# Hybrid mLSTM and neighbourhood-attention block on one core: low parts by accumulating DMAs and no elementwise work on POOL, from w_b to the feed forward

## The chip, the cores and the metric

The kernel runs on one core of one Trainium2 chip. The metric is device time in microseconds for one execution of the whole program, as the median of the executions shown. A core has TensorE (PE; its weight loads are listed as PEld), VectorE (DVE), ScalarE (ACT), GpSimd (POOL) and SyncE (SP), and DMA queues that SP and POOL issue to. All of them run on their own and wait for each other through semaphores.

## The reference, cut to what matters

One encoder layer on 1024 tokens of width 1024 and 16 meta tokens ahead of them. The projection `u = rms_norm(h) @ w_in` feeds two mixers, a bidirectional mLSTM (result y_a, 1024 wide) and a neighbourhood attention (result y_b, 512 wide), and the gates g_a and g_b. The change touches what comes after:

```python
mix = g_a * (y_a @ w_branch_a) + g_b * (y_b @ w_branch_b)
h = h + mix @ w_out
z = rms_norm(h, norm2_g) @ w_ff1            # 1024 -> 4096
h = h + jnp.square(jax.nn.relu(z)) @ w_ff2  # 4096 -> 1024
```

Everything is float32.

## The kernel before

**Three products for one.** Each operand of a matmul is kept as a high part, a copy rounded to the format of the fast matmul, and a low part, the operand less its high part. `mm3` multiplies high by high, high by low and low by high into one PSUM bank. The helper `hilo` makes both parts: ACT copies the high part, and `rest` subtracts it from the source on VectorE or POOL, whichever a running account of both (`either`, with the weight `share_gp`) calls free sooner. `gp_helps` allows POOL in this choice; it is false until the mixers are done and true from there on. In the mixers and in `Weights`, for w_in and w_b, low parts are made otherwise: ACT copies the high part with its sign turned, and a DMA issued by POOL adds the source to it in place.

**Stages.** They run in this order: w_b (eight column blocks `w_b[j]`, 24 matmuls each, by `gemm_in`, with the evacuation `ev_b` on VectorE, which multiplies by the gate tile gbq); w_a (four objects `Cols`, `cols_a`); w_out (one object `Rows`, `out_p`); w_ff1 (sixteen `Cols`, `cols_1`); w_ff2 (four `Rows`, `rows_2`). `Cols` and `Rows` form each product of 2 by 2 blocks with seven block products in place of eight, so sums and differences of blocks are made first. The blocks of the activations are A11, A12, A22 and the sums S1 to S4 (`s_parts`); for w_a they are the y operands, 14 pairs of high and low tiles of 128 x 1024. `ASIDE` says which one belongs to which of the seven products. A `Cols` step is 12 matmuls with 512 columns, a `Rows` step 24. A column of `Cols` reads its weights into two raw tiles (r0, r1), for w_a from a pool of three buffers ("wr"), and makes seven parts c1 to c7 of them, each 512 columns high and 512 low.

**Order.** The list `seq` holds all steps. For each step `ensure` first prepares operands up to `ah` steps ahead (`AH1` is 5, in w_out `AH2` is 2), and hooks in `before` issue loads. In the first ten steps of w_ff1 (the products 1 and 2 of five columns, `NE2`), which use the first half of the activations only, the look-ahead shrinks to the last of these steps. The second half, h21 and h22, passes norm2, the transposes `zt` and `s_parts` in that time. The tile framework schedules the instructions of each engine with a timeline of its own, so an instruction may stand earlier than its place in the program. Nearly all tiles are slots of one pool of 44 (`NSLOT`).

**Around the change.** `load_gb` reads the gate tiles gbq back from DRAM for w_b; ev_b's result goes to DRAM (gbd) and is read again as gba for w_a's evacuation `out_a`. The evacuation of w_ff1, `out_1`, adds two results and then takes max(z, 0) * z in one VectorE instruction. The weights of w_out are the tiles wo; their parts are called pow01 to pow17, those of the mix poz01 to poz17 (quarter, then product). Parts of w_a are wa0c to wa3c, of w_ff1 w10c to w115c. Most instructions are issued by the wrapper in line 137 and so carry this line.

Of the kernel before, what the change touches and what calls it, by code (L numbers as in the profile page):

```python
# [17 lines left out]
S = 1024  # L18
# [164 lines left out]
def build(tc, A, taps=None):  # L183
# [49 lines left out]
    def rest(out, src, part, bulk=1.0):  # L233
        either(free(out), bulk).tensor_sub(out, src, part.bitcast(F32))
# [879 lines left out]

    W.split_to(([*w_ga.values()] + w_b)[GS])
    nsp.close()
    gp_helps[0] = True
    LP = ctx.enter_context(tc.tile_pool(name="late", bufs=1))

    def late(name, dt=F32):  # L1120
# [13 lines left out]
    def add(out, a, b):  # L1134
        either(free(out), share_gp[0]).tensor_add(out, a, b)

    def hilo(src, name):
        h_, l_ = slot(name + "h", F32R), slot(name + "l", F32R)
        SC.copy(h_[:, 0:S], src[:, 0:S])
        rest(l_[:, 0:S], src[:, 0:S], h_[:, 0:S], share_gp[0])  # L1140
        return h_, l_


    gbd = dp.tile([4, 2, 128, 1024], F32, name="gbd")
    ybs = []
    for j in range(8):
        if f"ga{j}" not in F.done:
            F.add(f"ga{j}", job_ga(j), GE)
    for u in range(4):
        F.fill(12)  # L1150
        ybs.append(hilo(yb[u], f"yb{u}"))
    while F.jobs:
        F.fill(12)

    gb = {}

    def load_gb(p):
        for h_ in range(2):
            gb[p, h_] = slot(f"gbq{p}{h_}")
            dma(gb[p, h_][:, 0:1024].rearrange("p (e t) -> p e t", e=2),  # L1160
                gated[2 * p:2 * p + 2, :, h_ * 512:h_ * 512 + 512].rearrange("e p t -> p e t"))

    def ev_b(j):
        def ev(b, n0, n, ps):
# [10 lines left out]

    ASIDE = {1: "A11", 2: "A12", 3: "S4", 4: "A22", 5: "S1", 6: "S2", 7: "S3"}

    def s_parts(q, z, name):

        s1 = [slot(f"{name}s1{i}") for i in range(2)]  # L1180
        for i in range(2):
            add(s1[i][:, 0:S], q[1, i][:, 0:S], q[1, 2 + i][:, 0:S])
            z["S1", i] = hilo(s1[i], f"{name}s1{i}")
        yield
        for i in range(2):
            a11, a21 = q[0, i], q[1, i]
            sub(a21[:, 0:S], a11[:, 0:S], a21[:, 0:S])
            sub(a11[:, 0:S], s1[i][:, 0:S], a11[:, 0:S])
            z["S2", i] = hilo(a11, f"{name}s2{i}")
        yield  # L1190
        for i in range(2):
            z["S3", i] = hilo(q[1, i], f"{name}s3{i}")
        yield
        for i in range(2):
            z["A22", i] = hilo(q[1, 2 + i], f"{name}a22{i}")
        yield
        for i in range(2):
            sub(q[0, 2 + i][:, 0:S], q[0, 2 + i][:, 0:S], q[0, i][:, 0:S])
            z["S4", i] = hilo(q[0, 2 + i], f"{name}s4{i}")
        yield  # L1200

    LATE_C = (("w10", 1), ("w10", 2), ("w11", 1))
# [1 line left out]
    class Cols:  # L1204


        def __init__(self, name, src, z, out, raw_slot):
            self.name, self.src, self.z, self.out, self.raw_slot = name, src, z, out, raw_slot
            self.r, self.c, self.t = {}, {}, {}
            self.gen = self.parts()  # L1210

# [5 lines left out]
                self.r[e] = t  # L1217
            return self.r[e]

        def part(self, i, src):  # L1220
            c = late("c", F32R) if (self.name, i) in LATE_C else slot(f"{self.name}c{i}", F32R)
            SC.copy(c[:, 0:512], src)
            rest(c[:, 512:1024], src, c[:, 0:512], share_gp[0])
            self.c[i] = c

        def parts(self):
            e = self.raw(0)
            b11, b21 = e[:, 0:512], e[:, 512:1024]
            self.part(1, b11)
            yield  # L1230
            self.part(2, b21)
            yield
            o = self.raw(1)
            b12, b22 = o[:, 0:512], o[:, 512:1024]
            tt = late("tt")
            t1, t2 = tt[:, 0:512], tt[:, 512:1024]
            sub(t1, b12, b11)
            sub(t2, b22, t1)
            self.part(6, t2)
            yield  # L1240
# [49 lines left out]
    class Rows:  # L1290


        def __init__(self, name, quarters, out, tmp):
            self.name, self.quarters, self.out, self.tmp = name, quarters, out, tmp
            self.q, self.z, self.w = {}, {}, {}
            self.gen = {}

# [3 lines left out]

        def part(self, q, i, a, b, da=None, db=None):
            self.z[q, i] = self.split(a, da, f"{self.name}z{q}{i}")
            self.w[q, i] = self.split(b, db, f"{self.name}w{q}{i}")

        def split(self, t, src, name):
            if src is None:
# [8 lines left out]
        def parts(self, q):  # L1316
            self.load(q)
            c = slice(0, 1024)
            (a11, a12, a21, a22), (b11, b12, b21, b22) = [[t[:, c] for t, _ in x] for x in self.q[q]]
            (_, _, _, d22), (_, _, e21, e22) = [[src for _, src in x] for x in self.q[q]]  # L1320
            self.q[q] = None
            self.part(q, 1, a11, b11)
            yield
            self.part(q, 2, a12, b21, None, e21)
            yield
            s1, t1 = self.tmp("s1")[:, c], self.tmp("t1")[:, c]
            add(s1, a21, a22)
# [52 lines left out]
    def out_a(p):  # L1380
        def out(h_, e, ps, addend):
            g, b = ga[p, h_][:, lo(e)], gb[p, h_][:, lo(e)]
            c = cols_a[p].spare()[:, 512:1024]
            V.tensor_add(c, ps, addend)
            V.scalar_tensor_tensor(g, g, 1.0, c, OP.add, OP.mult)
            V.scalar_tensor_tensor(g, b, 2.0, g, OP.mult, OP.add)
        return out

    cols_a = [Cols(f"wa{p}", A["w_a"][2 * p:2 * p + 2], za, out_a(p), False) for p in range(4)]
    sy = s_parts(yq, za, "y")  # L1390
    NBS = ((0, 512), (512, 512))
    load_gb(0)
    for j in range(8):
        if j == 7:
            cols_a[0].prep(2, 0)
        if j % 2 == 0 and j < 6:
            load_gb(j // 2 + 1)
        run(gemm_in(w_b[j], NBS, ev_b(j), 4, ([t[0] for t in ybs], [t[1] for t in ybs])))
        if j in (1, 2):
            load_ya(j - 1)  # L1400
        if j in (3, 4):
            for i in (0, 1):
                za["A11" if j == 3 else "A12", i] = hilo(yq[0, 2 * (j - 3) + i], f"ya{j}{i}")
        if j >= 5:
            next(sy)
    ybs = None
# [31 lines left out]
    def out_quarters(q):  # L1438
        a = [(ga[p, h_], None) for p, h_ in ((q, 0), (2 + q, 0), (q, 1), (2 + q, 1))]
        b = []  # L1440
        for kh in range(2):
            for ch in range(2):
                t = slot(f"wo{q}{kh}{ch}")
                dma(t[:, 0:1024], A["w_out"][kh * 2 + q, ch])
                b.append((t, None))
        return a, b

    def load_x2(t):
# [38 lines left out]
        dma(h2d[t * 128:(t + 1) * 128, :], hx[t][:, 0:D])  # L1487
        norm2(t)

    out_p = Rows("po", out_quarters, out_o, late)  # L1490


    z2d = dp.tile([16, 2, 128, 1024], F32, name="z2d")
# [1 line left out]
    def out_1(p):  # L1495
        zq, cnt = {}, [0, 0]

        def out(h_, e, ps, addend):
            if h_ not in zq:
                zq[h_] = slot(f"zq{p}{h_}")  # L1500
            o = zq[h_][:, lo(e)]
            V.tensor_add(o, ps, addend)
            V.scalar_tensor_tensor(o, o, 0.0, o, OP.max, OP.mult)
            cnt[h_] += 1
            if cnt[h_] == 2:
                dma(z2d[p, h_], zq.pop(h_)[:, 0:1024])
        return out
# [77 lines left out]
    def hook(d, n, fn):  # L1585
        d.setdefault(n, []).append(fn)
# [41 lines left out]
        hook(before, n_1 + 2 * k + 3, lambda: next(sz))  # L1628
    for p in range(16):
        n = next(k for k, x in enumerate(seq) if x[0] is cols_1[p] and x[1] == (6 if p < NE2 else 1))  # L1630
        hook(before, n - 7 if p >= NE2 else max(n - 5, n_1 + 2 * NE2), lambda p=p: (cols_1[p].raw(0), cols_1[p].raw(1)))
    for g in range(1, NG):
        for q in range(2):
            hook(before, n_2 + 14 * g - 7 + 3 * q, lambda g=g, q=q: rows_2[g].load(q))
# [3 lines left out]
    for n, (o, i, q) in enumerate(seq):  # L1638
        for fn in before.get(n, ()):
            fn()  # L1640
        share_gp[0] = 1e6 if n >= n_2 - 8 else BULK if n >= n_1 + 2 * NE2 + 14 else 1.5 if n < n_1 else 1.0
        ah = AH3 if n >= n_2 else AH2 if n_o <= n < n_1 - 6 else AH1
        if n_1 <= n < n_1 + 2 * NE2:
            ah = n_1 + 2 * NE2 - 1 - n
        ensure(n + ah, n)
        o.mul(i, q)
    ctx.close()
# [69 lines left out]
```

## Time and profile before

| | us |
|---|---|
| median of 3 runs | 1671.81 (1669.5 to 1674.51) |
| profiled execution, its own time | 1675.85 |
| its span, first to last instruction | 1674.1 |
| TensorE busy | 1607.5 (96%) |
| VectorE busy | 1187.1 (71%) |
| ACT busy | 805.4 (48%) |
| POOL busy | 421.9 (25%) |
| mean granted TensorE clock | 0.984 |

The profile is of one execution. Its times count from the first instruction. Busy shares are means over stages that differ, so a stage is read from a stretch of the span. A matmul's record overlaps the next one's, so a busy TensorE can still lose time to a lower clock; matmuls in a stretch are counted for that.

### The profile page before, as it was taken

What the parts mean: (1) busy time and instruction counts of PE and PEld (TensorE: products, weight loads), DVE (VectorE), ACT (ScalarE), POOL (GpSimd) and SP (SyncE); (2) the same over time, 40 slices, a digit from 0 to 9 for tenths busy, and PEclk for the clock granted to TensorE, in tenths of its full rate; (3) what the DMA queues carried; (4) which work ended last, traced back from release to release, by engine and by line L of the source; (5) the groups of instructions that cost most, each with busy time, mean ns of one, the idle gap of its engine ahead of it and who ended that gap; (6) DMA issues with size and microseconds to landing.
All of it is one profiled execution on the core that took longest, in us unless ns stands there. A gap on an engine that the chain in (4) does not pass through costs nothing.

```text
span 1674.1 us, 22348 instructions
## 1 busy us (share of the span) xinstructions
PE 1607.5 (96%) x8009; PEld 1360.8 (81%) x8009; DVE 1187.1 (71%) x2156; ACT 805.4 (48%) x1418; POOL 421.9 (25%) x480
## 2 busy tenths in 40 slices
PE   6999899999999999999899889799999999999999
PEld 6978789888989989888678668588888887888887
DVE  3537666474757786873588998986667686869597
ACT  5466676576737676753232345322222237353450
POOL 5010212122133313212467565640000000010100
PEclk9999999999999999999999999899999999999999
DMA  6252754636274534446835311033223558281823
GB/s 204 59 133 64 159 135 128 138 87 163 55 188 89 120 69 102 91 105 174 256 106 215 112 70 69 25 137 127 101 101 126 195 170 269 58 264 53 237 77 100
DMA packets 76687, 214.77 MB, mean 128 GB/s; under 512 B 11145, under 2 KB 21769, under 8 KB 76577
## 3 DMA queue, kind: packets, MB, share of 16 engines
q1 hardware_dynamic: 54688, 137.71, 23.6%
q0 software_dynamic: 21888, 75.64, 21.7%
q8 instruction: 63, 1.03, 0.2%
q14 instruction: 48, 0.39, 0.1%
HBM read 166.02 MB, written 38.76 MB: 122 GB/s over the span
## 4 chain that ended last, share of the span: by engine, by line
PE 75%; DVE 9%; DMA 6%; issue 5%; ACT 4%; POOL 1%; SPq 0%; POOLq 0%; DVEq 0%; ACTq 0%
PE pf L137 38%; PE g L137 26%; DMA wl<-w_in 3%; PE po L137 2%; PE pt L137 1%; DVE ga L137 1%; PE pp L137 1%; PE ps L137 1%; PE pu L137 1%; PE pi L137 1%; PE pn L137 1%; DMA gbd<-gbq 1%; DVE zq L137 1%; DVE gt L137 1%; DMA xcl<-xc 1%
## 5 line engine op out<-in xcount | busy, mean ns | idle before, releaser
L137 PE MATMUL g<-xh,wh 128*128 128x512 f32 (+3 forms) x832 | 308.2, 371 | 8.2 <-ACT xm L137 3.0
L137 PE MATMUL g<-xh,wl 128*128 128x512 f32 (+3 forms) x832 | 298.0, 366 | 8.4 <-DMA wl<-w_in 8.4
L137 PE MATMUL g<-xl,wh 128*128 128x512 f32 (+3 forms) x832 | 303.7, 365 | 0.0
L137 PEld LDWEIGHTS g<-xh,wh 128*128 128x128 f32 x832 | 159.5, 192 | 26.7 <-ACT xm L137 3.8
L137 PEld LDWEIGHTS g<-xh,wl 128*128 128x128 f32 x832 | 157.6, 191 | 28.7 <-DMA wl<-w_in 10.3
L137 PEld LDWEIGHTS g<-xl,wh 128*128 128x128 f32 x832 | 159.7, 192 | 16.8
L137 DVE TENSOR_TENSOR acc<-acc,pf 128x512 f32<-128x512 f32 x96 | 64.3, 684 | 39.3 <-PE pf L137 39.2
L174 POOL DMA_DIRECT2D wl<-w_in x44 | 40.5, 920 | 162.4 <-ACT wl L137 71.9
L137 DVE CUSTOM_DVE_ANT_0 P<-ps,bt 128x400 f32<-128x400 f32 x64 | 36.1, 570 | 43.4 <-PE pp L137 20.9
L137 ACT ACTIVATE wl<-wh 128x1024 fp32r<-128x1024 f32 (+1 forms) x52 | 51.4, 989 | 24.7 <-PE g L137 11.6
L137 ACT COPY pu<-pf 128x512 f32<-128x512 f32 x20 | 11.7, 585 | 105.6 <-PE pf L137 105.6
L137 DVE SCALAR_TENSOR_TENSOR C<-C,decb,pu 128x258 f32<-128x258 f32 x52 | 23.7, 479 | 38.0 <-PE pu L137 37.6
L137 DVE SCALAR_TENSOR_TENSOR zq<-zq 128x512 f32<-128x512 f32 x64 | 47.5, 744 | 0.6
L137 ACT ACTIVATE P<-P,mn 128x400 f32<-128x400 f32 x64 | 40.3, 630 | 12.9 <-DVE mn L137 12.4
L137 DVE TENSOR_TENSOR pu<-pf,pu 128x512 f32<-128x512 f32 x40 | 27.3, 684 | 20.6 <-PE pf L137 20.5
L161 POOL DMA_DIRECT2D wh<-w_in x44 | 29.7, 676 | 44.8 <-PE pk L137 16.5
L137 DVE TENSOR_TENSOR zq<-pf,pu 128x512 f32<-128x512 f32 x32 | 22.0, 687 | 25.1 <-PE pf L137 25.1
L137 DVE TENSOR_SCALAR P<-P,sm 128x384 f32<-128x384 f32 (+1 forms) x128 | 38.6, 365 | 0.9
L137 DVE TENSOR_TENSOR zq<-pf,sp 128x512 f32<-128x512 f32 x32 | 22.0, 687 | 22.6 <-PE pf L137 22.4
L137 DVE TENSOR_TENSOR ptl<-pp,pth 128x384 fp32r<-128x384 f32 x64 | 35.5, 555 | 2.6 <-ACT pth L137 1.7
L137 POOL COPY bt<-mbias 128x32 f32<-128x32 f32 x32 | 8.3, 260 | 113.2 <-DVE mn L137 113.1
L137 ACT CAST pth<-pp 128x512 fp32r<-128x512 f32 x60 | 34.0, 581 | 5.4 <-PE pp L137 5.2
(2398 smaller groups left out, 4893.9 us busy)
## 6 DMA issues: line engine op xcount, KB each, us to landing
wh<-w_in POOLq DMA_DIRECT2D x44, 512.0 KB, 5.4
wl<-w_in POOLq DMA_DIRECT2D x44, 512.0 KB, 6.4
z2d<-zq SPq DMA_DIRECT2D x32, 512.0 KB, 3.6
zr<-z2d SPq DMA_DIRECT2D x32, 512.0 KB, 4.5
w2r<-w_ff SPq DMA_DIRECT2D x32, 512.0 KB, 13.2
bt<-rpbd SPq DMA_DIRECT2D x256, 32.0 KB, 2.8
xcl<-xc POOLq DMA_DIRECT2D x8, 520.0 KB, 5.2
ra<-rowd SPq DMA_DIRECT2D x8, 512.0 KB, 4.5
```

The source lines that it names most:

```text
L137: return fn(out, *a, **k)
L161: self.nc.gpsimd.dma_start(h[:, 0:src.shape[-1]], src)
L174: self.nc.gpsimd.dma_start(l[:, 0:w], src, accum_op=OP.add)
```

## The change

From w_b on POOL no longer takes part in additions and subtractions: `gp_helps` stays false, so `either` always answers VectorE. The low parts of the 14 y operands, of all parts of w_a and of all weight parts of w_out are made by ACT (copy of the high part with its sign turned) and an accumulating DMA that POOL issues, from SBUF or, where the tile is changed later, from DRAM. The squares of w_ff1 become two ACT passes. The gate tiles are loaded earlier: the first pair before the last jobs of the mixers, the others one block sooner. The raw tiles of the first two columns of w_ff1 are hooked 6 and 3 steps sooner, and in the early steps of w_ff1 at least two steps are prepared ahead. The low parts of the yb operands, of the mix, of z and of w_ff1 stay subtractions, now on VectorE.

```diff
-    gp_helps[0] = True
...
-    def hilo(src, name):
+    def hilo(src, name, by_dma=False):
         h_, l_ = slot(name + "h", F32R), slot(name + "l", F32R)
         SC.copy(h_[:, 0:S], src[:, 0:S])
-        rest(l_[:, 0:S], src[:, 0:S], h_[:, 0:S], share_gp[0])
+        low(l_[:, 0:S], src[:, 0:S], h_[:, 0:S], by_dma)
         return h_, l_
 
+    def low(l_, src, h_, by_dma):
+        if by_dma:
+
+            SC.activation(l_, h_.bitcast(F32), AF.Copy, scale=-1.0)
+            nc.gpsimd.dma_start(l_, src, accum_op=OP.add)
+        else:
+            rest(l_, src, h_, share_gp[0])
...
+    load_gb(0)
+    while F.jobs:
+        F.fill(12)
...
-        def part(self, i, src):
+        def part(self, i, src, dram=None):
             c = late("c", F32R) if (self.name, i) in LATE_C else slot(f"{self.name}c{i}", F32R)
             SC.copy(c[:, 0:512], src)
-            rest(c[:, 512:1024], src, c[:, 0:512], share_gp[0])
+            low(c[:, 512:1024], src if dram is None else dram, c[:, 0:512], self.by_dma)
...
-            self.w[q, i] = self.split(b, db, f"{self.name}w{q}{i}")
+            self.w[q, i] = self.split(b, b if self.by_dma and db is None else db, f"{self.name}w{q}{i}")
...
-    cols_a = [Cols(f"wa{p}", A["w_a"][2 * p:2 * p + 2], za, out_a(p), False) for p in range(4)]
-    sy = s_parts(yq, za, "y")
+    cols_a = [Cols(f"wa{p}", A["w_a"][2 * p:2 * p + 2], za, out_a(p), False, True) for p in range(4)]
+    sy = s_parts(yq, za, "y", True)
     NBS = ((0, 512), (512, 512))
-    load_gb(0)
+    load_gb(1)
...
-        if j % 2 == 0 and j < 6:
-            load_gb(j // 2 + 1)
+        if j in (1, 3):
+            load_gb(j // 2 + 2)
...
-                za["A11" if j == 3 else "A12", i] = hilo(yq[0, 2 * (j - 3) + i], f"ya{j}{i}")
+                za["A11" if j == 3 else "A12", i] = hilo(yq[0, 2 * (j - 3) + i], f"ya{j}{i}", True)
...
-    out_p = Rows("po", out_quarters, out_o, late)
+    out_p = Rows("po", out_quarters, out_o, late, True)
...
-            V.scalar_tensor_tensor(o, o, 0.0, o, OP.max, OP.mult)
+            SC.activation(o, o, AF.Relu)
+            SC.activation(o, o, AF.Square)
...
-        hook(before, n - 7 if p >= NE2 else max(n - 5, n_1 + 2 * NE2), lambda p=p: (cols_1[p].raw(0), cols_1[p].raw(1)))
+        hook(before, n - 7 if p >= NE2 else max(n - 5, n_1 + 2 * NE2 - (6 if p == 0 else 3 if p == 1 else 0)), lambda p=p: (cols_1[p].raw(0), cols_1[p].raw(1)))
...
-            ah = n_1 + 2 * NE2 - 1 - n
+            ah = max(n_1 + 2 * NE2 - 1 - n, 2)
```

## Rows read from the trace of the kernel before

**Rows 1.** The page: busy time, DMA queues, costliest groups (busy us, mean ns | idle).

```profile
PE 1607.5 (96%) x8009; PEld 1360.8 (81%) x8009; DVE 1187.1 (71%) x2156; ACT 805.4 (48%) x1418; POOL 421.9 (25%) x480
...
q1 hardware_dynamic: 54688, 137.71, 23.6%
q0 software_dynamic: 21888, 75.64, 21.7%
...
L174 POOL DMA_DIRECT2D wl<-w_in x44 | 40.5, 920 | 162.4 <-ACT wl L137 71.9
...
L137 ACT ACTIVATE wl<-wh 128x1024 fp32r<-128x1024 f32 (+1 forms) x52 | 51.4, 989 | 24.7 <-PE g L137 11.6
...
L137 DVE SCALAR_TENSOR_TENSOR zq<-zq 128x512 f32<-128x512 f32 x64 | 47.5, 744 | 0.6
```

**Rows 2.** Busy time by stretch: us, each engine, PEclk, DMA share, GB/s.

```profile
791.84:846.28 54.44, 48.96 (x193) 37.37 (x192) 29.14 (x28) 15.99 (x20) 26.07 (x18) 0.94 0.73 230
846.28:866.83 20.55, 20.25 (x86) 15.40 (x85) 18.97 (x16) 8.69 (x13) 14.18 (x9) 1.00 0.51 176
866.83:925.17 58.34, 58.34 (x253) 47.33 (x252) 51.76 (x55) 15.09 (x25) 40.41 (x23) 1.00 0.51 189
925.17:1026.81 101.64, 90.97 (x373) 70.91 (x372) 94.75 (x83) 44.64 (x59) 63.02 (x36) 0.93 0.20 75
1026.81:1082.32 55.51, 45.60 (x185) 34.64 (x184) 49.95 (x39) 23.16 (x34) 34.16 (x21) 0.88 0.10 38
1082.32:1380.00 297.68, 297.68 (x1288) 241.69 (x1287) 217.60 (x318) 73.61 (x123) 40.08 (x27) 1.00 0.38 135
```

**Rows 3.** The chain that ended last, transposes at the end of w_out (start, us, what).

```profile
1012.30 2.62 PE pt L137 x24
```

**Rows 4.** Waits of TensorE from 791.84 to 1083 (us in total, times, longest).

```profile
PE pf L137 <- DVE zq L137: 5.7, 2, 3.6
...
PE pf L137 <- ACT w10c L137: 2.9, 1, 2.9
```

**Rows 5.** Timeline of POOL and VectorE in w_out (start, us, what).

```profile
938.18 2.42 POOL L137 TENSOR_TENSOR pow12l<-wo,pow12h 128x1024 fp32r<-128x1024 f32 x1 [6.50 <-ACT pow12h L137]
...
936.54 1.22 DVE L137 TENSOR_TENSOR pow11l<-wo,pow11h 128x1024 fp32r<-128x1024 f32 x1
...
938.27 3.41 DVE L137 TENSOR_TENSOR pow02l<-wo,pow02h 128x1024 fp32r<-128x1024 f32 x1
```

**Rows 6.** Timeline of TensorE, ACT, VectorE and SP's queue in w_out and w_ff1.

```profile
934.71 0.47 PE L137 MATMUL pf<-pow02h,poz02h 128*128 128x512 f32 x1 [2.85 <-DVE sp L137]
...
924.76 1.05 ACT L137 CAST pow11h<-wo 128x1024 fp32r<-128x1024 f32 x1 [6.19 <-DMA wo<-w_out]
...
1070.54 0.68 DVE L137 TENSOR_TENSOR tt<-w10r,tt 128x512 f32<-128x512 f32 x1
...
1056.35 0.33 SPq L1216 DMA_DIRECT2D w10r<-w_ff  x1
```

**Rows 7.** DMA queues and issues, 452 to 459 us, then 834.5 to 840.5.

```profile
q0 software_dynamic: 144, 0.52, 46.6%
...
wl<-w_in POOLq DMA_DIRECT2D x1, 512.0 KB, 5.5
...
q0 software_dynamic: 144, 0.26, 29.8%
...
wl<-w_b POOLq DMA_DIRECT2D x1, 256.0 KB, 4.0
```

**Rows 8.** Timeline of ACT, SP's queue, VectorE and TensorE in w_a.

```profile
875.25 1.14 ACT L137 CAST wa1c<-wa1r 128x512 fp32r<-128x512 f32 x2 [2.46 <-DVE ga L137]
...
878.16 0.33 SPq L1216 DMA_DIRECT2D wa2r<-w_a  x1
...
885.36 1.18 DVE L137 TENSOR_TENSOR wa2c<-tt,wa2c 128x512 fp32r<-128x512 f32 x1
...
889.04 0.39 PE L137 MATMUL pf<-ys20h,wa2c 128*128 128x512 f32 x1
```

More of the change, by code (lines that the diff above doesn't have):

```diff
@@ L1148, in build @@
             F.add(f"ga{j}", job_ga(j), GE)
[L1149 to L1153, printed above, removed]
     gb = {}
@@ L1161, in load_gb @@
                 gated[2 * p:2 * p + 2, :, h_ * 512:h_ * 512 + 512].rearrange("e p t -> p e t"))
+    for u in range(4):
+        F.fill(12)
+        ybs.append(hilo(yb[u], f"yb{u}"))
+    load_gb(0)
+    while F.jobs:
+        F.fill(12)
     def ev_b(j):
@@ L1176, in build, with s_parts @@
     ASIDE = {1: "A11", 2: "A12", 3: "S4", 4: "A22", 5: "S1", 6: "S2", 7: "S3"}
-    def s_parts(q, z, name):
+    def s_parts(q, z, name, by_dma=False):
         s1 = [slot(f"{name}s1{i}") for i in range(2)]
@@ L1182, in s_parts @@
             add(s1[i][:, 0:S], q[1, i][:, 0:S], q[1, 2 + i][:, 0:S])
-            z["S1", i] = hilo(s1[i], f"{name}s1{i}")
+            z["S1", i] = hilo(s1[i], f"{name}s1{i}", by_dma)
         yield
@@ L1188, in s_parts @@
             sub(a11[:, 0:S], s1[i][:, 0:S], a11[:, 0:S])
-            z["S2", i] = hilo(a11, f"{name}s2{i}")
+            z["S2", i] = hilo(a11, f"{name}s2{i}", by_dma)
         yield
         for i in range(2):
-            z["S3", i] = hilo(q[1, i], f"{name}s3{i}")
+            z["S3", i] = hilo(q[1, i], f"{name}s3{i}", by_dma)
         yield
         for i in range(2):
-            z["A22", i] = hilo(q[1, 2 + i], f"{name}a22{i}")
+            z["A22", i] = hilo(q[1, 2 + i], f"{name}a22{i}", by_dma)
         yield
@@ L1198, in s_parts @@
             sub(q[0, 2 + i][:, 0:S], q[0, 2 + i][:, 0:S], q[0, i][:, 0:S])
-            z["S4", i] = hilo(q[0, 2 + i], f"{name}s4{i}")
+            z["S4", i] = hilo(q[0, 2 + i], f"{name}s4{i}", by_dma)
         yield
@@ L1204, in build, with __init__ @@
     class Cols:
-        def __init__(self, name, src, z, out, raw_slot):
+        def __init__(self, name, src, z, out, raw_slot, by_dma=False):
             self.name, self.src, self.z, self.out, self.raw_slot = name, src, z, out, raw_slot
+            self.by_dma = by_dma
             self.r, self.c, self.t = {}, {}, {}
@@ L1230, in parts @@
             yield
-            self.part(2, b21)
+            self.part(2, b21, self.src[0][:, 512:1024] if self.by_dma else None)
             yield
@@ L1290, in build, with __init__ @@
     class Rows:
-        def __init__(self, name, quarters, out, tmp):
+        def __init__(self, name, quarters, out, tmp, by_dma=False):
             self.name, self.quarters, self.out, self.tmp = name, quarters, out, tmp
+            self.by_dma = by_dma
             self.q, self.z, self.w = {}, {}, {}
@@ L1319, in parts @@
             (a11, a12, a21, a22), (b11, b12, b21, b22) = [[t[:, c] for t, _ in x] for x in self.q[q]]
-            (_, _, _, d22), (_, _, e21, e22) = [[src for _, src in x] for x in self.q[q]]
+            (_, _, _, d22), (e11, _, e21, e22) = [[src for _, src in x] for x in self.q[q]]
             self.q[q] = None
-            self.part(q, 1, a11, b11)
+            self.part(q, 1, a11, b11, None, e11 if self.by_dma else None)
             yield
@@ L1443, in out_quarters @@
                 t = slot(f"wo{q}{kh}{ch}")
-                dma(t[:, 0:1024], A["w_out"][kh * 2 + q, ch])
-                b.append((t, None))
+                src = A["w_out"][kh * 2 + q, ch]
+                dma(t[:, 0:1024], src)
+                b.append((t, src))
         return a, b
```

## The prediction

> **What bounds the kernel now.** The page comes first: TensorE is busy for 96% of the span [rows 1], so a change can only win where it waits or runs slowly. The view of busy time by stretch finds these places. The last three columns of w_a are the yardstick: 21 steps of 12 matmuls, 252 in all, take 58.34 us, 0.2315 us each [rows 2]. At that rate the 192 matmuls of w_b need 44.4 us and take 54.4: 10.0 lost. The first column of w_a (84 matmuls, 19.4 us) takes 20.55: 1.1 lost. The stretch of w_out holds 340 matmuls (78.7 us) and some 32 transposes at about 0.11 us (3.4) [rows 2, 3] and takes 101.6: 19.5 lost. The start of w_ff1 (152 matmuls, 35.2 us, and 32 transposes, 3.4) takes 55.5 at a granted clock of 0.88: 16.9 lost. From 1082 to 1380 TensorE never idles. Together 47.5 us are lost in what the change touches, and that is the most it can give.
>
> Why it is lost: the list of TensorE's waits is headed by VectorE [rows 4], and in the stretch of w_out VectorE is busy for 94.8 of 101.6 us [rows 2]. That is not work: where POOL runs beside it, VectorE's instructions with two SBUF operands stretch until POOL's end. A subtraction of 1024 columns takes 1.22 us alone and 3.41 when POOL starts one of its own, of 2.42, just before it [rows 5]: the two run one behind the other. So POOL's help makes the pair slower than VectorE alone, two low parts in 3.4 us against two in 2.4.
>
> **The change, part by part.** *POOL's additions and subtractions move to VectorE*, at 1.22 us for 1024 columns [rows 5] and 0.68 for 512 [rows 6]. VectorE's load then, counted in the code: w_b has 16 gate products of 0.68 and 8 sums of 1.22, 20.6 us of 44. A column of w_a has 15 evacuations and products of 0.69 and 4 differences, 13 us of 19.4. w_out has 16 sums and 14 low parts of 1.22, 32 evacuations of 0.68, 12 sums of 0.69 and 8 scalings of about 0.75 to 1.1: 73 us of 82. Its 14 other low parts would add 17 and make it 90; the DMAs take these away. The start of w_ff1 has 8 sums, 14 low parts, 10 halves and some scalings and evacuations, about 56 of 67 us. So VectorE has room in every stage, least in w_out (89%).
>
> *w_out:* 19.5 lost. The wait at 934.71 for VectorE's sp shows it 9 us behind on w_a's last column [rows 6]; without the stretching it is not behind. I keep 4 us for the first w_out low parts (the tile of pow11 is cast only at 924.76 [rows 6] and its low part would come some 8 us after that, while its step is due 5.6 us after the stretch begins at 925.17) and 3 for order: 7 left, a gain of 12.5. Bounds: 0, if 89% is as bad as 100%, and 17.
>
> *Start of w_ff1:* 16.9 lost. It ends in a wait of 2.9 us for w10c [rows 4], whose first difference VectorE makes only at 1070.54 [rows 6], because the early steps let no later part be prepared and w10's second tile is issued at 1056.35 [rows 6]. The change issues it six steps (16.7 us) sooner, prepares two steps ahead, and takes five squares (3.5 us) and the stretching (3.4 for 1.2, six times or so) from VectorE. I keep 3.5 lost, a gain of 13.4; bounds 6 and 16.
>
> *Low parts by DMA, w_b and w_a.* One low part was a subtraction of 1.2 us; now it is an ACT copy with sign (0.99 for 1024 columns), a POOL issue of 0.92 [rows 1] and a landing after 5.5 us (512 KB) or 4.0 (256 KB) [rows 7]: some 7 us more delay. With five steps (13.9 us) of preparation that alone is covered, but not the DMA engines' time. An accumulating DMA of 512 KB with nothing beside it held 46.6% of 7 us, 3.3 us of all engines; one of 256 KB 29.8% of 6, 1.8 us; over the whole span queue 0 moved 75.64 MB in 21.7% of the span, 2.5 us for 512 KB [rows 1, 7]. Until w_a's first column can end, 14 operand parts and 7 of its own must land: 14 x 3.3 + 7 x 1.8 = 59 us, or 44 by the cheaper rate. These 75 us of w_b and that column hold 0.73 x 54.4 + 0.51 x 20.6 = 50 us of DMA already [rows 2], so 25 are free. The stretch would become 19 to 34 us longer, if all of the old traffic went first. Fourteen transfers of it (eight gate writes, four gate reads, two tiles of w_a, about 1.4 us each, 20 us) may go behind, which brings the low end to no loss against before. I take 8 us longer: near the low end, since the two queues share and the gate tiles come sooner, but not at it. Bounds: 34 longer; and 9 shorter if VectorE's waits go and the DMAs hide.
>
> The Trainium skill, DMA: Bandwidth & Descriptors, section "Anatomy of one DMA", gives 2.0 us plus the bytes at 436 GB/s: 1.2 us of movement for 512 KB, so the 14 and 7 would take an estimated 21 us and hide in the 25. The trace disagrees: 3.3 us, and a landing after 5.5 where the rule gives 3.2. By the rule the stage would give 9 us and the sum would be some 17 better; the row decides.
>
> *w_a's other columns:* 21 parts need 26 to 38 us against 29 free [rows 2]. Their raw tiles rotate through three buffers and are now held until the DMA has read them: the second tile of column 2 is issued at 878.16, 2.9 us after the cast at 875.25; now about 6 after it. The part made from it was ready at 886.5 and used at 889.04 [rows 8]; it now comes 3 us later and takes 4 longer, less 2 for what VectorE does faster. I take 1 us for each of three columns, 3 in all; bounds 0 and 12.
>
> *Squares on ACT:* two passes of about 0.6 us (two casts of that width take 1.14 [rows 8]) for one of 0.74 [rows 1]. In the steady part of w_ff1 TensorE waits for nothing (297.68 of 297.68 [rows 2]), so 47 us off VectorE are worth nothing there, and ACT (73.6 of 297.7) has room for 77 more. At the end of w_ff1 the last z may land later: 0.5 taken, bounds 0 and 2.
>
> *Sum:* -12.5 - 13.4 + 8 + 3 + 0.5 = -14.4. The profiled execution took 1675.85 us (span 1674.1), 4 above the median of 1671.81; it becomes 1661.5, the median **1657**.
>
> **Rivals.** (1) *The DMAs hide:* if an accumulating transfer costs what a plain one does (queue 1: 137.71 MB in 23.6% of the span, 1.5 us for 512 KB [rows 1]), 14 and 7 need 26 us for 25 free. Then w_b gives 9 and w_a loses nothing: -35, **1637**. Against it stand the 3.3 us. (2) *The DMA queues become the bound, slower:* all old traffic stays ahead, w_a's first column ends 34 us later and the raw tiles cost 9: +43 - 26 + 0.5, **1689**. It decides once more than 26 us are lost there. For it: the DMA share is 0.73 already in w_b. Against it: TensorE's order can be filled with the next column's steps. (3) *VectorE stays the bound in w_out:* its 89% in a fixed order stalls as before: +8 + 3 + 0.5 - 13.4 = -2, **1670**.
>
> **How the numbers follow.** Chances: forecast 0.45 (its own range 1645 to 1667), hidden 0.27, DMA-bound 0.16, VectorE-bound 0.12. About 0.3% (5 us) is what a measurement here can tell from no change, so faster means under 1667 and slower over 1677. Faster: 0.43 + 0.27 + 0.03 = 0.73. Same: 0.02 of the forecast and 0.07 of VectorE-bound, 0.09. Slower: 0.16 + 0.02, 0.18. The range 1634 to 1684 leaves out some 0.05 below and 0.13 above.
>
> **What would show it.** Right: in w_out VectorE's 1024-column subtractions at 1.2 us throughout, TensorE waiting under 8 us there, and no wait for w10c; in w_b a DMA share near 1 up to the first column of w_a, with TensorE's waits now for DMA landings of ys and ya parts. Wrong: subtractions still stretched (then POOL's DMA issues lock too), waits in w_a's later columns for wa tiles, or a share well under 1 in w_b with no wait, which is rival 1.

## The result and the profile after

The changed kernel takes 1683.21 us (median of 4 runs, 1680.5 to 1685.16), the kernel before in the same session 1670.93 (4 runs, 1669.5 to 1674.51): a ratio of 1.0069, 95% interval 1.0054 to 1.0084. It is 12 us slower, where 1657, 14 us faster, was forecast. Its profiled execution took 1684.36 us, with a span of 1682.6 us, 8.5 more than before.

Of the page after, the busy times, the DMA queues and the squares, beside [rows 1]:

```profile
PE 1601.6 (95%) x8009; PEld 1357.6 (81%) x8009; DVE 1091.3 (65%) x2134; ACT 926.7 (55%) x1607; POOL 270.4 (16%) x433
...
q0 software_dynamic: 29952, 97.66, 28.7%
q1 hardware_dynamic: 54688, 137.71, 23.7%
...
L137 ACT ACTIVATE zq<-zq 128x512 f32<-128x512 f32 x128 | 80.7, 633 | 124.1 <-DVE zq L137 122.3
```

POOL is relieved of 151 us and VectorE of 96, and the time did not follow. Queue 0 moves 22 MB more (14 operand parts of w_a and 14 weight parts of w_out of 512 KB, 28 parts of w_a of 256 KB), and its share rises from 21.7% of 1674.1 us to 28.7% of 1682.6: 120 us of all 16 engines, 2.8 for each 512 KB.

Busy time by stretch after, columns as in [rows 2] (w_b, w_a, w_out, the start of w_ff1, its rest):

```profile
789.41:851.99 62.58, 49.65 (x193) 38.27 (x192) 19.90 (x24) 23.77 (x29) 15.24 (x19) 0.89 0.97 256
...
789.41:959.28 169.87, 136.89 (x532) 105.30 (x531) 71.21 (x98) 70.06 (x99) 44.87 (x53) 0.89 0.95 241
...
959.28:1048.57 89.29, 84.76 (x373) 68.74 (x372) 69.13 (x88) 57.40 (x72) 19.20 (x25) 0.96 0.67 172
...
1048.57:1104.23 55.66, 53.31 (x243) 42.13 (x241) 49.79 (x65) 39.38 (x63) 2.21 (x4) 1.00 0.18 67
1104.23:1380.00 275.77, 275.77 (x1192) 223.69 (x1191) 168.56 (x255) 135.36 (x226) 1.77 (x2) 1.00 0.38 136
```

w_b takes 62.58 us (54.44 before), and w_b with w_a, the second row, 169.87 (133.33 before). Part of these 37 us is idle time of TensorE, 33.0 now and 5.8 before. The rest is that its matmuls are slower: 532 records keep it busy for 136.89 us, at a granted clock of 0.89, where before 529 took 127.55 at 0.97. The DMA share of the whole stretch is 0.95. Behind it the sizes of the forecast hold: w_out, with the same 373 records, takes 89.29 us (101.64; three more of its matmuls, 0.7 us, now stand ahead of the last ten of w_a), and of the 55.66 us at the start of w_ff1 the 211 matmuls and 32 transposes account for 52.2, so 3.4 are lost there (16.9 before).

TensorE's waits after, from 789.41 to 1104 (us in total, times, longest), beside [rows 4]:

```profile
PE g L137 <- DMA wl<-w_b: 11.4, 2, 9.9
PE pf L137 <- ACT wa0c L137: 11.2, 3, 4.3
PE pf L137 <- DMA wa3c<-tt: 5.4, 1, 5.4
PE pf L137 <- ACT pow02h L137: 4.5, 1, 4.5
```

The waits for VectorE's zq and for w10c are gone. In their place stand a low part of w_b, which the change didn't touch, and the parts of w_a. The first of them can be followed through the timelines of ScalarE, POOL and TensorE (start, us, what, the wait before it):

```profile
823.29 1.06 ACT L137 ACTIVATE ya41l<-ya41h 128x1024 fp32r<-128x1024 f32 x1 [8.48 <-DVE yq L137]
825.78 0.63 ACT L137 ACTIVATE wl<-wh 128x512 fp32r<-128x512 f32 x1 [1.43 <-DMA gbd<-gbq]
...
825.10 0.55 POOL L161 DMA_DIRECT2D wh<-w_b  x1 [9.96 <-DVE yq L137]
825.75 0.88 POOL L1146 DMA_DIRECT2D ya41l<-yq  x1
826.81 0.88 POOL L174 DMA_DIRECT2D wl<-w_b  x1 [0.19 <-issue]
...
835.00 0.79 PE L137 MATMUL g<-yb0h,wl 128*128 128x512 f32 x1 [9.94 <-DMA wl<-w_b]
```

ScalarE stands for 8.48 us before ya41l and POOL for 9.96 before the next high part of w_b. Neither reads what VectorE computes there: both are about to write a tile that takes one of the 44 slots, and I read both waits as waits for a slot, which ends when VectorE has read an old tile for the last time. The low part of w_b is then issued at 826.81, lands 8 us later, and TensorE waits 9.94 us for it. Two explanations fit, and the experiments go by them. **T1:** the 16 engines' time is the bound (share 0.95). **T2:** order and slots; a low part made by a DMA holds its source and its target among the 44 slots until it lands, and what stands behind it on ScalarE and POOL is late.

### The profile page after: what moved, and what is told of

It reads as the page before. It is cut to its first block, busy times and chain, and to the rows that moved or that the text cites. A ratio compares the mean times of both kernels' runs of the same rounds, so it can differ in the third digit from the quotient of the medians.

```text
span 1682.6 us, 22476 instructions
## 1 busy us (share of the span) xinstructions
PE 1601.6 (95%) x8009; PEld 1357.6 (81%) x8009; DVE 1091.3 (65%) x2134; ACT 926.7 (55%) x1607; POOL 270.4 (16%) x433
## 3 DMA queue, kind: packets, MB, share of 16 engines
q0 software_dynamic: 29952, 97.66, 28.7%
## 5 line engine op out<-in xcount | busy, mean ns | idle before, releaser
L137 ACT ACTIVATE zq<-zq 128x512 f32<-128x512 f32 x128 | 80.7, 633 | 124.1 <-DVE zq L137 122.3
L137 ACT ACTIVATE wl<-wh 128x1024 fp32r<-128x1024 f32 (+1 forms) x52 | 51.3, 989 | 19.3 <-DMA wh<-w_b 8.6
L137 DVE SCALAR_TENSOR_TENSOR gbq<-gbq,g 128x512 f32<-128x512 f32 x16 | 11.0, 685 | 46.6 <-PE g L137 46.6
## 6 DMA issues: line engine op xcount, KB each, us to landing
w2r<-w_ff SPq DMA_DIRECT2D x32, 512.0 KB, 13.2
```

Source lines behind the costliest of these rows:

```text
L137: return fn(out, *a, **k)
```

## Experiments

The numbers are the order of the labels; they stand here by what they tell. "w_b and w_a" is in each the stretch from the first matmul of w_b to the first of w_out: 133.33 us before, 166.88 after (789.41 to 956.29). Where w_a's parts go by DMA (after and experiments 1, 5 to 8, 10 and 13 to 17), the first three matmuls of w_out stand ahead of the last ten of w_a, so the stretch leaves out 2.3 us (10 x 0.2315) that it holds in the other kernels; a comparison of one kind with the other adds them. How far profiles of the same code differ can be seen twice. Experiments 3, 11 and 12 have the same code in w_b and w_a and take 129.02, 131.11 and 131.00 us there. After and the eleven experiments just named have the same code from w_out on and take 722.13 to 726.94 us from its first matmul to the end. The expectations speak of 16 operand transfers; there are 14 (A11, A12, A22, S1 to S4, two each).

**1 to 4 and 9: which part of the change costs, which gains.** Experiment 1 makes the operands' low parts on VectorE again:

```diff
-    sy = s_parts(yq, za, "y", True)
+    sy = s_parts(yq, za, "y")
...
-                za["A11" if j == 3 else "A12", i] = hilo(yq[0, 2 * (j - 3) + i], f"ya{j}{i}", True)
+                za["A11" if j == 3 else "A12", i] = hilo(yq[0, 2 * (j - 3) + i], f"ya{j}{i}")
```

> The kernel after, but the low parts of the eight operands of w_a (16 of 512 KB) are subtractions on VectorE again; w_a's own and w_out's low parts stay DMAs. Theory T1 (the time of the accumulating DMAs on the 16 engines is the bound of w_b and of w_a's first column): the 16 DMAs cost some 3.3 us of all engines each, 53 us of movement go, w_b comes back to about 10 us lost (18 now) and w_a's first column gives 8 to 15 back: 1658 to 1665. Theory T2 (each low part now holds its slots until its DMA lands, ScalarE waits for a slot, and behind it in ScalarE's and POOL's order w_b's own low parts are late): the same gain in w_b, but w_a keeps the most of its 29 us, because its parts are still chains of copy, copy and DMA: 1668 to 1675.

Measured: 1657.01 us, ratio to before 0.9923 (0.99 to 0.9946). 26 us come back, 11.3 in w_b (51.3) and the rest in w_a. That is T1's total or a little more (1658 to 1665); T2 had left most of w_a's loss in place.

Experiment 2 makes w_a's own low parts on VectorE again:

```diff
-    cols_a = [Cols(f"wa{p}", A["w_a"][2 * p:2 * p + 2], za, out_a(p), False, True) for p in range(4)]
+    cols_a = [Cols(f"wa{p}", A["w_a"][2 * p:2 * p + 2], za, out_a(p), False) for p in range(4)]
```

> The kernel after, but the low parts of w_a (28 of 256 KB) are subtractions on VectorE again; the low parts of its operands and w_out's stay DMAs. T1: of the movement in the crowded stretch only the seven parts of the first column go (about 12 us of all engines), and w_b keeps its 18 us lost: 1665 to 1675. T2: w_b keeps its 18 us, w_a's first column still waits for the operands, and of the 29 us lost in w_a some 15 to 20 go: 1662 to 1670. Either way this tells how the 29 us of w_a divide between its own parts and its operands.

Measured: 1661.13 us, 0.9943 (0.9922 to 0.9963): 22 us, of which w_a gives 20 (86.7 us, against 104.3 and the 2.3 left out there); w_b keeps 60.4. T1's range is missed, and T2's is met at its low end. T1 had counted the seven parts of the first column only, but the DMA share is 0.94 through all of w_a; experiment 10 tells movement from the chain of each part.

Experiment 3 is both edits.

> The kernel after, with the low parts of w_a and of its operands both as subtractions on VectorE; only w_out's stay DMAs, POOL does no elementwise work, squares on ScalarE and the hooks stay. If the failed step of the forecast is the low parts by DMA in w_b and w_a (about 35 us by the trace) and the gains of 26 us in w_out and at the start of w_ff1 are independent of it, w_b loses about 8 to 12 us and w_a 1 to 4, and the time is 1645 to 1652, the best so far. Rival: without POOL and without the DMAs VectorE (35 us more of subtractions at 1.22 and 0.65 us between 790 and 950) becomes the bound of w_b and w_a: 1660 to 1670.

Measured: 1641.59 us, 0.982 (0.9797 to 0.9842), 29 us faster than before. Busy time by stretch, w_b and w_a, of experiments 1 and 3:

```profile
787.15:927.10 139.95, 124.70 (x520) 97.34 (x519) 83.99 (x109) 55.60 (x85) 32.77 (x39) 0.99 0.84 232
```

```profile
786.56:915.58 129.02, 124.05 (x530) 98.48 (x528) 101.42 (x138) 40.55 (x57) 8.27 (x11) 1.00 0.60 206
```

With all 42 low parts on VectorE this engine is busy for 101 of 129 us and is no bound; TensorE idles for 5 us and has its full clock (1.00). So the two sets of transfers cost 40 us of stretch (166.88 and 2.3 against 129.02) and 42 of total. The gains elsewhere don't need them.

Experiment 4 is meant to take the transfers from w_out too, on top of experiment 3. Experiment 9 is the other end: the kernel before, with one line gone.

```diff
-    out_p = Rows("po", out_quarters, out_o, late, True)
+    out_p = Rows("po", out_quarters, out_o, late)
```

```diff
-    gp_helps[0] = True
```

> The third experiment's kernel (1641.6 us) with w_out's 14 low parts as subtractions on VectorE too, so that no low part is newly made by a DMA; POOL does no elementwise work. If w_out's gain comes from the low parts by DMA (my step: VectorE is w_out's bound without them), 14 x 1.22 = 17 us come on top of VectorE's 69 in w_out's 89 us, and 8 to 17 us are lost there: 1650 to 1659. If it comes from POOL's no longer stretching VectorE, under 4: 1640 to 1646.

> The kernel before with POOL's elementwise help from w_b on taken away (one line), and nothing else. If POOL's port contention (VectorE 3.41 us where it takes 1.22 alone) is the greater part of the loss in w_b and w_out, this alone gains 8 to 18 us: 1653 to 1663. If VectorE needs the help, it becomes the bound in w_out and in the start of w_ff1: 1672 to 1690. The difference between this and the fourth kernel of this call is then what the hooks, the squares and the gates' loads bring together, about 13 us by the forecast.

(In the last sentence of the second, the other kernel meant is experiment 4.) Experiment 4 does less than its expectation says. `split` makes a low part by DMA wherever it is given a source in DRAM, and the edit leaves these sources in place, so four of the 14 low parts (pow02, pow12, pow03, pow13) still go by DMA. Two of these in the timeline of POOL, and the longest of TensorE's waits in w_out:

```profile
920.23 0.86 POOL L1323 DMA_DIRECT2D pow02l<-w_out  x1 [91.58 <-ACT pow02l L137]
...
964.93 0.86 POOL L1323 DMA_DIRECT2D pow13l<-w_out  x1 [7.22 <-ACT pow13l L137]
...
PE pf L137 <- DMA pow13l<-w_out: 3.1, 1, 3.1
```

The kernel with all 14 on VectorE is experiment 9, in the old order. Measured: experiment 4 1643.7 us, 0.984 (0.9814 to 0.9866); experiment 9 1649.79, 0.9871 (0.9847 to 0.9896). The one line alone gains 1.3%. Busy time from the first matmul of w_out to the end, of before, experiments 9, 4 and 3:

```profile
925.17:1674.10 748.93, 722.96 (x3089) 580.92 (x3087) 589.50 (x696) 269.69 (x350) 156.39 (x104) 0.98 0.39 126
```

```profile
917.33:1646.50 729.17, 714.31 (x3089) 576.36 (x3087) 574.78 (x751) 272.28 (x355) 29.29 (x40) 0.99 0.40 129
```

```profile
915.37:1641.90 726.53, 713.21 (x3089) 575.39 (x3087) 534.12 (x683) 352.31 (x487) 31.98 (x44) 1.00 0.42 133
```

```profile
915.58:1638.90 723.32, 711.89 (x3089) 575.38 (x3087) 523.80 (x674) 360.77 (x496) 42.37 (x53) 1.00 0.45 140
```

Read down the first column: ending POOL's help brings 19.8 us here, with VectorE's busy time falling by 15 although it executes 55 instructions more. The further steps, 2.6 from 9 to 4 and 3.2 from 4 to 3, are smaller than profiles of the same code differ here (4.8). Two parts of this stretch tell more: w_out alone (101.64 us before), and the start of w_ff1 up to the first matmul on w10c. First the start of w_ff1 in the kernel before, then both parts in experiments 9 and 3:

```profile
1026.81:1071.98 45.17, 35.26 (x149) 26.90 (x148) 40.82 (x34) 17.83 (x27) 23.85 (x14) 0.89 0.12 47
```

```profile
917.33:1007.99 90.66, 86.23 (x373) 68.42 (x372) 84.85 (x103) 44.63 (x59) 6.80 (x12) 0.96 0.23 84
1007.99:1044.40 36.41, 31.28 (x149) 24.67 (x147) 31.60 (x38) 20.33 (x32) 1.53 (x4) 1.00 0.16 58
```

```profile
915.58:1005.40 89.82, 85.75 (x376) 69.17 (x375) 70.44 (x90) 57.56 (x72) 19.30 (x25) 0.96 0.67 168
1005.40:1037.39 31.99, 30.58 (x147) 24.25 (x145) 26.98 (x32) 23.70 (x38) 2.21 (x4) 1.00 0.19 66
```

Ending POOL's help alone gives w_out 11.0 us. All 14 low parts are then VectorE's, which is busy for 84.85 of 90.66 us, and with the transfers w_out is not measurably shorter (89.82). At the start of w_ff1 it gives 8.8 us, and the other edits 4.4. In w_b and w_a experiment 9 needs 127.25 us, 6 less than before.

**5 to 8: movement or order.** Experiment 5 puts the gate loads back to where they were before:

```diff
-    load_gb(0)
...
-    load_gb(1)
+    load_gb(0)
...
-        if j in (1, 3):
-            load_gb(j // 2 + 2)
+        if j % 2 == 0 and j < 6:
+            load_gb(j // 2 + 1)
```

> The kernel after, with the loads of the gates at their old places (one column pair ahead, issued after blocks 0, 2 and 4 of w_b) instead of ahead of w_b; all else stays. T1: the same bytes move, no change: 1680 to 1686. T2: the loads ahead hold two more of the 44 slots through w_b, and each of the waits of ScalarE and POOL for a slot there comes earlier to its end: 4 to 9 us faster, 1674 to 1679. A third outcome, slower by 2 to 5, if a gate load now ends a wait of VectorE in w_b as it did before.

Measured: 1684.77 us, 1.0086 (1.0066 to 1.0107), w_b 62.76: the gate loads ahead are neither the cost nor a gain. Experiment 8 splits w_b's weights a block sooner:

```diff
-        run(gemm_in(w_b[j], NBS, ev_b(j), 4, ([t[0] for t in ybs], [t[1] for t in ybs])))
+        run(gemm_in(w_b[j], NBS, ev_b(j), 4, ([t[0] for t in ybs], [t[1] for t in ybs]), ahead=2))
```

> The kernel after, with w_b's weights split two blocks ahead of the running one instead of one; nothing else. T1: the same bytes have to move, so what w_b gains (its waits of 9.9 and 1.5 us for a low part of w_b), the operands' low parts lose: the sum of w_b and w_a stays within 4 us, 1680 to 1688. T2: the waits for w_b's weights go and nothing comes back, 8 to 11 us faster, 1672 to 1675. A third: two more slots are held, and ScalarE's waits for a slot grow, slower by 3 to 10.

Measured: 1685.05 us, 1.0078 (1.0052 to 1.0104). w_b gains 6.9 us (55.69) and w_b with w_a stays at 166.76 (166.88 in after): what the weights win, the operands lose. This is T1's answer. Experiment 6 copies instead of adding, experiment 7 adds 64 of 1024 columns, both in the operands' transfers alone:

```diff
-            nc.gpsimd.dma_start(l_, src, accum_op=OP.add)
+            nc.gpsimd.dma_start(l_, src)
```

```diff
-            nc.gpsimd.dma_start(l_, src, accum_op=OP.add)
+            nc.gpsimd.dma_start(l_[:, 0:64], src[:, 0:64], accum_op=OP.add)
```

> The kernel after, but the 16 transfers that make the low parts of w_a's operands don't accumulate: each copies its 512 KB over the negated high part. The computation of these low parts is left out (they hold the whole value); the instructions, their order, the queue and the slots stay as in after. T1 (the 16 engines' time is the bound): an accumulating 512 KB took 3.3 us of all engines where it was alone, a plain one about 1.4 in the trace; some 16 x 1.9 = 30 us of movement go, and of the 26 us that the first experiment gave, 15 to 26 come here: 1657 to 1668. T2 (the order of the queue and of the slots: a low part stands between a block of w_b and its weights whatever it moves): under 8 us come, 1675 to 1684.

> The kernel after, but each of the 16 transfers for the operands' low parts adds only the first 64 of 1024 columns (32 KB in place of 512): the rest of these low parts is left out. Number, order, queue, slots and ScalarE's copies stay. T1 (the engines' time): nearly all of the 26 us of the first experiment come, 1656 to 1662. T2 (what plain transfers left, 12 us above the first experiment, is order, slots and a landing that no size shortens): 1665 to 1671.

Measured: 1668.66 us, 0.9981 (0.9966 to 0.9996), and 1668.18, 0.9973 (0.9957 to 0.9989). The share of queue 0 and the landing of three operand parts (the last column, us), from the DMA view of w_b and w_a, of after and of experiment 6, and the share in experiment 7:

```profile
q0 software_dynamic: 7839, 18.09, 58.9%
...
ys11l<-ys POOLq DMA_DIRECT2D x1, 512.0 KB, 4.8
ys20l<-yq POOLq DMA_DIRECT2D x1, 512.0 KB, 4.6
ys31l<-yq POOLq DMA_DIRECT2D x1, 512.0 KB, 9.1
```

```profile
q0 software_dynamic: 7920, 18.35, 53.1%
...
ys11l<-ys POOLq DMA_DIRECT2D x1, 512.0 KB, 2.9
ys20l<-yq POOLq DMA_DIRECT2D x1, 512.0 KB, 2.9
ys31l<-yq POOLq DMA_DIRECT2D x1, 512.0 KB, 5.3
```

```profile
q0 software_dynamic: 7920, 11.47, 43.6%
```

Times the stretch's length, queue 0 holds all engines for 98 us in after, 82 in experiment 6 and 67 in experiment 7. The first 16 us of movement less are worth 12.1 us of the stretch (154.75), the next 15 nothing (154.27). So T1 holds for 12 of the 27 us by which experiment 1 is shorter, and 14 are something else.

**13 to 17: what the rest is.** Experiments 13 and 14 turn the operands' signs on VectorE, 13 on top of experiment 7 and 14 on after:

```diff
-            SC.activation(l_, h_.bitcast(F32), AF.Copy, scale=-1.0)
+            V.tensor_scalar(l_, h_.bitcast(F32), -1.0, None, OP.mult)
```

> The seventh experiment's kernel (1668.2 us; of each of the 16 low parts only 64 columns are added, the rest is left out), with the 16 sign-turning copies of 1.06 us on VectorE instead of ScalarE. T2 in its new form (ScalarE's order: 16 x 1.06 = 17 us of these copies stand ahead of the copies of w_a's first column, which start only at 857 us there, and TensorE waits 5.3 us for them): most of the 11 us still missing to the first experiment come, 1657 to 1662. Rival (it is the slots, or the landing itself behind every low part): 1665 to 1671.

> The kernel after (1683.2 us, nothing left out), with the same 16 copies on VectorE; the transfers add all columns. If the two costs of the operands' transfers add (about 15 us for the engines' time, 11 for ScalarE's order), 1670 to 1675. If the accumulating transfers' time is the bound whatever ScalarE does, 1680 to 1685: the copies only waited for what the transfers held up anyway.

Measured: 1668.3 us, 0.9976 (0.996 to 0.9992), and 1682.73, 1.0053 (1.003 to 1.0076). Taking the copies off ScalarE gains nothing, and this form of T2 falls. (In the profile of 13 the stretch is 4.0 us shorter than in that of 7, but 3.4 are lost behind it.) Experiments 15 (on 7) and 16 (on after) put the first parts of w_a ahead in the queues:

```diff
-        if j == 7:
+        if j == 4:
             cols_a[0].prep(2, 0)
```

> The seventh experiment's kernel (1668.2 us, of each of the 16 low parts of w_a's operands only 64 columns are added, the rest is left out), with the first two parts of w_a's first column prepared ahead of block 4 of w_b, not of block 7. T2 as POOL's and ScalarE's order (these two parts stood behind eight of the operands' in both queues and were issued 53 us after w_b's start, 47 in the first experiment): 5 to 10 us come, 1658 to 1663. If it is the slots and the landings behind the operands themselves: within 3, 1665 to 1671.

> The kernel after (1683.2 us, nothing left out), with the same two parts prepared ahead of block 4 of w_b. T1 (movement is the bound until the operands have landed): within 4 us, 1680 to 1687. Order as a cost of its own, that adds to movement: 1674 to 1679.

Measured: 1672.86 us, 1.0004 (0.9985 to 1.0023), and 1684.88, 1.0081 (1.0049 to 1.0114). No gain: the place of these parts isn't it either. Left were the slots. Experiment 17 is experiment 7 with two tiles moved out of the 44:

```diff
-        s1 = [slot(f"{name}s1{i}") for i in range(2)]
+        s1 = [(late if name == "y" else slot)(f"{name}s1{i}") for i in range(2)]
```

> The seventh experiment's kernel (1668.2 us, of each of the 16 low parts only 64 columns are added, the rest is left out), with the two sums s1 of the y quarters in the pool of seven single buffers that w_b doesn't use, so that two of the 44 slots come free in the second half of w_b. T2 as a wait for slots (there VectorE waits 6.9 us to write ys until a gate write lands, ScalarE 1 to 2 us several times): 4 to 10 us come, 1658 to 1664. If slots are not it, within 3: 1665 to 1671; then the 11 us stay open.

Measured: 1662.12 us, 0.9938 (0.9923 to 0.9953), 6 us faster than experiment 7. VectorE's first sum of the y quarters, in the timelines of experiments 7 and 17:

```profile
822.78 1.22 DVE L137 TENSOR_TENSOR ys<-yq,yq 128x1024 f32<-128x1024 f32 x1 [6.90 <-DMA gbd<-gbq]
```

```profile
805.74 1.22 DVE L137 TENSOR_TENSOR ys<-yq,yq 128x1024 f32<-128x1024 f32 x1
```

In 7 it begins 31.2 us after the first matmul of w_b (791.60), after a wait for a gate write that it doesn't read; I take it for a wait for that tile's slot, and the edit bears it out. In 17 it begins after 18.1 us (787.68) and waits for nothing. The stretch falls from 154.27 to 147.18 us (busy time of experiments 7 and 17 there):

```profile
791.60:945.87 154.27, 131.49 (x520) 101.66 (x518) 68.97 (x95) 69.98 (x99) 45.01 (x53) 0.93 0.83 218
```

```profile
787.68:934.86 147.18, 131.45 (x520) 102.88 (x518) 70.19 (x98) 70.13 (x99) 44.95 (x53) 0.92 0.87 223
```

TensorE's busy time is the same, its idle time 7.0 less. The 7 us that still divide 17 from experiment 1 are not idle time: TensorE idles for 15.7 us in 17 and for 15.3 in 1. Its 520 records take longer, 131.45 us against 124.70, at a granted clock of 0.92 against 0.99. Two neighbouring slices of 17 show it:

```profile
846.55:856.36 9.81, 4.83 (x11) 3.35 (x12) 1.49 (x3) 9.00 (x15) 4.37 (x5) 0.61 0.39 56
856.36:866.18 9.82, 9.82 (x31) 7.76 (x32) 2.14 (x4) 1.25 (x2) 3.48 (x4) 0.69 1.03 215
```

In the first TensorE is idle for half of the time; in the second it never idles, and does 31 matmuls, where such a slice holds 44 at a clock of 1.00. The longest waits are 5.0 and 4.0 us in 17 and 3.4 in 1. Why single waits are longer in 17 stays open. The edit of 17 was not tried on after itself; the changes of order that were (5, 8, 14 and 16) gave nothing.

**10: w_a's own parts**, on experiment 1, adding 64 of 512 columns in `Cols.part`:

```diff
-            nc.gpsimd.dma_start(l_, src, accum_op=OP.add)
+            nc.gpsimd.dma_start(l_[:, 0:64], src[:, 0:64], accum_op=OP.add)
```

> The first experiment's kernel (operands' low parts on VectorE, 1657.0 us), but each of the 28 transfers for w_a's low parts adds only the first 64 of 512 columns; the rest of them is left out. T1: the 15 us by which it is above the third experiment (1641.6) are the engines' time, DMA share 0.84 there: 1641 to 1647. T3 (they are the longer chain of each part: copy, copy with sign, issue, landing, and the raw tiles that it holds): the waits for parts made from tt and of the last columns stay, 1651 to 1658.

Measured: 1645.67 us, 0.9834 (0.9814 to 0.9853); w_b and w_a take 130.06 us at a DMA share of 0.67. Of the 13.2 us between experiments 1 and 3 (139.95 and 2.3 against 129.02) it gives 9.9 back, and T1's range holds: for these parts it is mostly movement, and 3 us are left.

**11, 12 and 18: the other edits**, on experiment 3: 11 has the squares in one VectorE instruction again, 12 the old hooks and look-ahead in w_ff1, and 18 the edit of experiment 17.

```diff
-            SC.activation(o, o, AF.Relu)
-            SC.activation(o, o, AF.Square)
+            V.scalar_tensor_tensor(o, o, 0.0, o, OP.max, OP.mult)
```

```diff
-max(n - 5, n_1 + 2 * NE2 - (6 if p == 0 else 3 if p == 1 else 0))
+max(n - 5, n_1 + 2 * NE2)
...
-            ah = max(n_1 + 2 * NE2 - 1 - n, 2)
+            ah = n_1 + 2 * NE2 - 1 - n
```

> The third experiment's kernel (1641.6 us) with the squares of w_ff1 back on VectorE, one instruction in place of two on ScalarE. My step said 0.5 us lost by the two passes, bounds 0 and 2, and 3.5 us of VectorE's time won in the first columns of w_ff1: if both hold, 1640 to 1645. If VectorE is the bound at the start of w_ff1 once it does POOL's work, 3 to 8 slower: 1645 to 1650.

> The third experiment's kernel (1641.6 us) with the two changes of order in w_ff1 undone (the raw tiles of its first two columns 6 and 3 steps sooner, and at least two steps prepared ahead). My step ascribed the 13.4 us won at the start of w_ff1 mainly to these, of which some 3 to 5 to the end of the stretching: if so, 8 to 10 us are lost, 1649 to 1652. If the end of POOL's help is the greater part, as the fourth kernel before this (1649.8 without any of the edits but that) suggests, 2 to 5: 1643 to 1647.

> The third experiment's kernel (1641.6 us, nothing left out), with the same two sums in that pool. w_b loses 6 us there, of which 3.2 are waits for VectorE's gate products, which stand behind the sums. If those sums wait for a slot, 2 to 4 us come: 1637 to 1640; if not, no change: 1640 to 1644.

(In the second, the kernel of 1649.8 us is experiment 9.) Measured: 1644.45 us, 0.9825 (0.9808 to 0.9842); 1646.86, 0.9837 (0.9811 to 0.9863); 1643.74, 0.9841 (0.9818 to 0.9864). From w_out to the end experiment 11 takes 722.60 us and experiment 12 727.29, against 723.32, differences that profiles of the same code show too. The squares make none that can be measured. For the order, the start of w_ff1 up to the first matmul on w10c tells more (experiment 12, and its wait there):

```profile
1011.55:1046.38 34.83, 30.61 (x146) 24.14 (x144) 28.71 (x33) 26.33 (x42) 2.21 (x4) 1.00 0.16 61
...
PE pf L137 <- ACT w10c L137: 2.8, 1, 2.8
```

It is 2.8 us longer than in experiment 3, which has no such wait. Two more slots don't help where no operand goes by DMA. No version beats experiment 3 measurably.

## Why the prediction was wrong

*The step that failed is "low parts by DMA, w_b and w_a", taken at 8 us longer.* With the 3 us of w_a's other columns it allowed 11; the profiles show 36.5 (169.87 against 133.33), and against experiment 3, where the same low parts are subtractions, 40. Divided at the last matmul of w_a's first column, after takes:

```profile
789.41:890.91 101.50, 75.20 (x280) 56.04 (x278) 28.01 (x37) 44.10 (x56) 28.21 (x34) 0.85 0.99 246
890.91:959.28 68.37, 61.69 (x254) 49.26 (x253) 43.20 (x62) 25.96 (x43) 16.67 (x20) 0.95 0.90 234
```

That is 26.5 us more than before (74.99) where 8 was taken, and 10.0 more (58.34) where 3 was taken.

Three things were wrong in it. First the choice: the working gave 19 to 34 us of movement above what was free, and I went under it by letting fourteen old transfers go behind. Most of them did not (SP's queue in after, and POOL's issue of the last low part of the first column):

```profile
798.65 54.57 SPq L1176 DMA_DIRECT2D gbd<-gbq  x8
857.38 2.80 SPq L1618 DMA_DIRECT2D gba<-gbd  x2
881.97 0.33 SPq L1225 DMA_DIRECT2D wa1r<-w_a  x1
883.60 0.33 SPq L1225 DMA_DIRECT2D wa2r<-w_a  x1
886.52 2.63 SPq L1618 DMA_DIRECT2D gba<-gbd  x2
...
879.50 0.89 POOL L1146 DMA_DIRECT2D wa0c<-wa0r  x1 [0.44 <-issue]
```

The eight gate writes and two of the gate reads were issued ahead of that low part, and only four transfers behind it. The price itself was right, 2.8 us for 512 KB by queue 0, between my 2.5 and 3.3: with it and no discount the working gives 24 us, near the 26.5. That it comes so near is in part luck, since movement is only 12 of the 27 us that the operands' transfers cost (experiments 6 and 7). The estimate from the Trainium skill, DMA: Bandwidth & Descriptors, section "Anatomy of one DMA" (1.2 us), disagrees with the trace for accumulating transfers: the 14 of the operands hold 31 us more in after than in experiment 7, at least 2.2 each. For plain copies it nearly agrees: in experiment 6 they hold 15 us more than in 7, 1.1 each. Second, the 44 slots were not in the sum: a tile is held until the transfer that reads or fills it has landed (the wait of 6.90 us in experiment 7), and two slots more gave 7 us in experiment 17, where the operands' transfers moved 32 KB each. Third, where TensorE waited its matmuls ran at a lower granted clock; these 133 us of the kernel before ran at 0.97, after at 0.89, which is 9 us of busy time for nearly the same matmuls. The last 7 us between experiments 17 and 1 are of this kind.

The measured time still lies in the stated range of 1634 to 1684, at its very end. That is no merit: the range was wide, and faster, which was given 0.73, did not come.

*w_out was right in size, and half wrong in reason.* 7 us lost were forecast and 89.29 less 82.1 is 7.2 (7.9 with the three matmuls that stand ahead). But I let the 14 transfers take 17 us from a VectorE that would else have more work than time; in experiment 9 all 14 are VectorE's, and w_out loses 8.6 (90.66). Rival 3, that 89% stalls, is refuted by the same row: there VectorE is busy for 94%.

*The start of w_ff1 was right in size, and its cause mis-sized:* 3.5 forecast, 3.4 measured. The forecast named the order first, and experiment 12's expectation gave it 8 to 10 us. Of the 13.2 us from 45.17 to 31.99, POOL's leaving brings 8.8 (experiment 9) and the order 2.8 (experiment 12).

*That POOL's help makes the pair slower* was right, and is the greater part of the gain: one line, 22 to 24 of the 29 us of experiment 3. *Squares on ACT* were right: 0.5 forecast, nothing measurable found. *Rival 1* fell (the transfers don't hide). *Rival 2* had the place and nearly the price (43 us, against 36.5), and was given 0.16; more than its 26 us were lost there. Its reason, the queues' time, holds for about half: 12 and 10 of the 40 us (experiments 6 and 10). Of the signs of being right, the share near 1 came, and w10c's wait went; of the signs of being wrong, a wait in a later column came (wa3c, 5.4 us). The first wait was for w_b's own weights, not for operands: whoever shares the queue and the slots is late, not only what the change touches.

## What to carry to other kernels

A change that takes one cost away and adds a replacement should be priced in two steps: here removing POOL's help was worth 1.3% alone, and the replacement for its work was needed nowhere, since VectorE without contention had time for all of it (101 of 129 us in w_b and w_a, 85 of 91 in w_out). An accumulating DMA isn't free arithmetic (2.2 to 2.8 us of all engines for 512 KB here): count its engine time against what the stage moves already, and count how long its source and target stay allocated, since the waits appear at whatever next needs a tile or that queue.

## What was not expected of the hardware

Cutting each of the 14 operand transfers from 512 to 32 KB gained nothing more than leaving off the accumulation: 1668.18 against 1668.66 us. Landing of a plain 512 KB from SBUF to SBUF took 2.9 us where the accumulating one took 4.6 to 4.8. And waits went with a second cost for TensorE. The first matmul after the wait of 9.94 us takes 0.79 us, where 0.39 is usual. With 33.0 us idle in w_b and w_a the granted clock was 0.89 and its busy time 136.89 us for 532 matmul records, with 5.0 idle 1.00 and 124.05 for 530.
